# Two gate chunks as a unit of seven products, branch products inside the last attention steps, and three reorderings

## The chip, the cores and the metric

One core of a Trainium2 chip runs the whole program in one launch. The metric is the device time in microseconds (us): the median of several runs. A profile of one further execution, taken by the hardware profiler, says what each engine did. The engines are TensorE (PE; its weight loads are listed as PEld), VectorE (DVE), ScalarE (ACT), GpSimdE (POOL) and SyncE (SP), whose queue issues nearly all transfers. Each engine works through its own list of instructions in order.

## The reference, cut to what matters

One layer of a streaming encoder, 1024 frames, width 1024, in float32:

```
h  = rmsnorm(x, norm_mix_g);  z = h @ w_in
qa, fa, ia, ga, qb, kb, vb, gate_a, gate_b = split(z)
oa = hgrn2_mixer(qa, fa, ia, ga, ...)                 # 4 heads of 128
ob = band_attention(qb, kb, vb, ...)                  # 8 heads of 64, a chunk of 64 frames sees itself and 8 before
merged = sigmoid(gate_a) * (oa @ w_branch_a) + sigmoid(gate_b) * (ob @ w_branch_b)
x = x + merged @ w_out
x = x + (silu(h2 @ w_ffn_gate) * (h2 @ w_ffn_up)) @ w_ffn_down      # h2 = rmsnorm(x)
x = x + sigmoid(h3 @ w_ple_gate) * (p @ w_ple_proj)                 # h3 = rmsnorm(x)
```

The two gates have 16 chunks of 128 columns together (0 to 7 for gate_a, 8 to 15 for gate_b).

## The kernel before, in words

**Number format.** Nearly every large product is made of three matrix products of split operands: a float32 tile is rounded to a short form (`hi`, a CAST on ACT) and the rest is kept (`lo`, a subtraction on DVE or POOL). `gemm` (line 102) issues hi times hi, hi times lo and lo times hi. A product of a weight chunk (128 columns) with an activation of 512 frames and K = 1024 is 8 x 3 = 24 matmuls of 128x512; with K = 512 (the branch products) it is 12.

**Stages.** `units` computes pairs of chunks of z by a scheme of seven half-size products instead of eight (`strassen`): 7 x 4 x 3 = 84 matmuls for two chunks and 1024 frames, where the plain way takes 96. The list `JOBS` says which chunks: pairs of gate chunks ('gate'), a head's q and f ('head') and output gates ('out'). The results of a gate unit get a sigmoid and are stored to DRAM (`gate_done`, `gate_keep`). Then `hgrn_mix` works on the first mixer while plain products (gate chunks 0, 1, 4, 5 and v) fill PE between its steps. Then comes `attention`, then `branches` (products with w_branch_a and w_branch_b, multiplied by gates), `out_proj`, the feed-forward stages and `ple`, whose end writes the output.

**The attention loop** has 32 steps n = 0 to 31 (a pair of heads and a block of 128 frames each) and two more to empty the pipeline. Even and odd n go over the two pairs of a half. In step n, in the order of the code:

- `stage(n-1, 1)`: the second head of the step before is normalized: RECIPROCAL and TENSOR_SCALAR on DVE.
- `next(feed)`: a filler, six 128x512 matmuls of other work.
- `scores(n)`: 12 matmuls of 64 rows for both heads, then on DVE four reductions with bias (the profile calls them CUSTOM_DVE_ANT_0, the program order ISA).
- `stack(n+1)`: two transposes for the next step, two ACTIVATEs on ACT and two SCALAR_TENSOR_TENSORs on DVE, which make q and k of scores(n+1).
- `next(feed)`: a second filler.
- in odd n, `pv(n-3)` and `pv(n-2)`: products with v (128*64 tiles), copied out by ACT.
- `pt(n-1, 1)`, `stage(n, 0)`, `stage(n, 1)` (the two Exp on ACT), `pt(n-1, 0)`, `stage(n, 0)` (RECIPROCAL on DVE, then a scaling ACTIVATE on ACT): pt is five transposes of the normalized scores and two copies of them, one by ACT and one by DVE.

The fillers are first the q, k projections of the attention itself (`attn_in`; 56 pulls are left when the loop begins, so that they last through n = 27), then gate chunks 2 and 3 in the plain way (`gate`, 16 pulls of six matmuls; 12 of them fall into n = 28 to 33). Operations through `self.V`, `self.A`, `self.G`, `self.load` and `self.mul` keep the order in which the code is written, engine by engine; each list is worked through in order.

**The branch products** need the first mixer's output, which was stored to DRAM: `branch_load` loads four tiles of 128x1024, `split` makes hi (ACT) and lo (DVE) of each. Before, `branch_first` does this from n = 32 on, beside the last gate fillers, and `branches` starts after them. `tile()` products of the first source are TENSOR_TENSORs with a gate tile loaded by `gate_load`.

**The last outputs**: in `ple`, `last(u, ps, sp)` takes the last product's four blocks, the fourth in two parts of 256 frames. `out` is a stream of steps: a multiplication by `rb` (DVE), a sigmoid (ACT), a multiplication (DVE), an addition (POOL, or DVE for the last part) and the store.

Of the kernel before, what the change touches and what calls it, by code (L numbers as in the profile page):

```python
# [24 lines left out]
STEPS = (NFF // 2 + 1) // 2  # L25
EPS = 1e-6
# [9 lines left out]
PLAIN = 6  # L36
FIRSTS = (0, 1, 4, 5)
JOBS = (('gate', 6), ('head', 1), ('gate', 8), ('head', 2), ('gate', 10), ('head', 3), ('gate', 12), ('gate', 14), ('out', 0), ('out', 2))
# [36 lines left out]
class Trunk:  # L75
# [532 lines left out]
    def attn_in(self):  # L608

        nc = self.nc  # L610
        late = []

        def scale():
            two, b, ps, ss = late.pop(0)
            qk = self.small(HALF, tag="qk")
            self.V.tensor_tensor(
                qk[:, :].rearrange("p (a d) -> p a d", d=64), ps[:, :].rearrange("p (a d) -> p a d", d=64),
                ss[:, :].unsqueeze(2).to_broadcast([P, 8, 64]), ALU.mult)
            for i in range(2):
                self.qk[2 * two + i, b] = qk[:, 256 * i:256 * i + 256]  # L620

        for two in range(2):
            ws = self.weights(4, ahead=0)
            for b in range(8):
                pss = []
                for n, _ in enumerate(self.tokens(ws, (b,), pss)):
                    if b == 7:
                        self.weights(0, ahead=n + 1 if two == 0 else 2, direct=True)
                    if n < 3:
                        yield 1296  # L630
                    if n == 0 and late:
                        scale()
                (ps,) = pss
                sq = self.small(HALF, tag="qk")
                self.A.activation(sq, ps, AF.Square)
                ss = self.small(8)
                self.V.tensor_reduce(ss, sq[:, :].rearrange("p (a d) -> p a d", d=64), axis=AX.X, op=ALU.add)
                self.V.tensor_scalar(ss, ss, 1.0 / 64, self.epsv[:, b:b + 1], ALU.mult, ALU.add)
                self.G.tensor_tensor(ss, ss, self.mhalf[:, 0:8], ALU.pow)
                late.append((two, b, ps, ss))  # L640
                yield 1296
        self.scale = scale
# [78 lines left out]
    def attention(self):  # L721
# [3 lines left out]
        feed = chain(self.feed, self.gate(ahead=3), self.gate(ahead=2))  # L725
# [38 lines left out]
        for n in range(whole + 2):  # L764
# [8 lines left out]
            drain(stack(n + 1))  # L773
            next(feed, None)
            if n % 2:
                pv(n - 3)
                pv(n - 2)
            pt(n - 1, 1)
# [11 lines left out]
            if n == whole:  # L790
                while self.queue:
                    self.rest()
                self.queue = None
                tail = self.branch_first()
            if n >= whole:
                next(tail)
            yield 0
        for x in feed:
            next(tail, None)
            yield x  # L800
        drain(tail)
        self.pinned = True


    def gate(self, ahead=AHEAD):
        (w,) = self.weights(1, ahead=ahead)
        t = self.slot()
        self.gates.append(t)
        for half in range(2):
            stream = self.feature(w, self.u, half, piece=2)  # L810
            if self.scale:
                yield next(stream)
                self.scale()
                self.scale = None
            ps = yield from stream
            hs = slice(half * HALF, half * HALF + HALF)
            self.nc.vector.tensor_tensor(t[:, hs], ps, self.rb[:, hs], ALU.mult)
            yield 1296
# [218 lines left out]
    def branch_first(self):  # L1037
        self.weights(0, ahead=3)
        raws = self.branch_load(self.od)
        yield  # L1040
        yield
        self.osrc = []
        for i, raw in enumerate(raws):
            self.osrc.append(self.split(raw))
            yield
        self.keep_heads(self.ob, self.obd, [2, 3])
        self.bgates = []
        self.gate_load()
        for t in self.gates:
            self.A.activation(t, t, AF.Sigmoid)  # L1050
        self.bgates += self.gates

    def gate_load(self):
        if len(self.bgates) < 2 * KC:
            for _ in range(2):
                t = self.slot(late=len(self.bgates) > 3)
# [3 lines left out]
    def branches(self):  # L1060
# [11 lines left out]
        for dd in range(4):  # L1072
# [6 lines left out]
            for i in range(2):  # L1079
                c = 2 * dd + i  # L1080
                for half in range(2):
                    hs = slice(half * HALF, half * HALF + HALF)
                    ps = yield from self.feature(w, src, half, off=i * HALF)
# [807 lines left out]
    def ple(self):  # L1891
# [53 lines left out]
        def last(u, ps, sp):  # L1945
            for _ in range(max(0, min(2, len(todo) - u))):
                drain(todo.pop(0))
            while u == 3 and todo:
                drain(todo.pop(0))
            stream = out(2 * u, h0, ps, V if u == 3 and sp.start else G, sp, late=False)  # L1950
            next(stream)
# [68 lines left out]
    def run(self):  # L2020
        tc, d = self.tc, self.d
        order = []
        order += [d["fm"][i] for i in range(2)] + [d["tm"][i] for i in range(4)] + [d["fm"][2 + c] for c in FIRSTS]
        order += [d["wv"][i] for i in range(4)]
        order += [d["qk"][i] for i in range(8)]
        order += [d["fm"][2 + c] for c in (2, 3)] + [d["ba"][i] for i in range(4)] + [d["bb"][i] for i in range(4)]
# [11 lines left out]
        with ExitStack() as es:  # L2038
# [9 lines left out]
            self.gates = []  # L2048
            self.hg, self.ended, self.pend, self.qk, self.bias, self.ob = {}, [], [], {}, {}, []
            self.oa = [None] * 4  # L2050
            with ExitStack() as xs:
# [24 lines left out]
            with ExitStack() as xs:  # L2076
                self.late = xs.enter_context(tc.tile_pool(name="late", bufs=6, reuse_waits="tile"))
                drain(self.branches())
# [109 lines left out]
def layout(i):  # L2188
# [7 lines left out]
    d["fm"] = np.concatenate([cq[:1], cf[:1], cz[:PLAIN]])  # L2196
# [48 lines left out]
```

## Time and profile before

| | |
|---|---|
| median of 3 runs | 1539.32 us (1539.03 to 1540.14) |
| profiled execution | 1538.07 us, its span 1536.3 us |
| PE busy | 1515.4 us (99%), 7704 matmuls |
| DVE, ACT, POOL busy | 1102.7, 660.7, 630.1 us |
| TensorE clock granted | 0.999 |
| steps n = 0 to 31 of the attention, start of scores | 432.21 us (n = 0) to 607.92 us (n = 31) |
| the last two products with v end the loop at | 620.77 us (start) |

The share of PE is nearly the whole span, but a matmul's end is modelled: one that is listed with 389 ns is followed by the next after some 227 ns, so short waits of 0.1 to 0.3 us between matmuls hide behind a "busy" PE. They show only in the distance between starts. Rows of the timeline below give the start, the duration, the engine, the line, the operation, and what it writes and reads; "x12" are so many instructions merged into one row.

### The profile page before, as it was taken

The numbers are of one execution on the slowest core, as the hardware profiler recorded it, in microseconds if no ns is written. First come the engines' busy times: TensorE is split into PE (matmuls) and PEld (weight loads), VectorE is DVE, ScalarE is ACT, GpSimd is POOL, SyncE is SP. The second block draws the span as 40 slices with busy tenths as digits, with TensorE's granted clock in tenths as the row PEclk, the third lists the DMA queues.
The fourth block names the chain that finished last, engine by engine and source line by source line (L and its number), as shares of the span: only waits on it lengthen the run. The fifth ranks groups of instructions, "written<-read, shape, count | busy, mean of one in ns | idle before, by whom it ended". The sixth has DMA issues, their size and how long they took to land.

```text
span 1536.3 us, 20676 instructions
## 1 busy us (share of the span) xinstructions
PE 1515.4 (99%) x7704; PEld 1248.4 (81%) x7704; DVE 1102.7 (72%) x1597; ACT 660.7 (43%) x1104; POOL 630.1 (41%) x349
## 2 busy tenths in 40 slices
PE   8999999999999999999999999999999999999998
PEld 6888888888777878888888888888888888888886
DVE  5777774776767667348888877777777667756678
ACT  6633333434367677412575322222222224456452
POOL 4243333010334222254203666665555545545446
PEclk9999999999999999999999999999999999999999
DMA  5544444798443434866345344443233288775325
GB/s 200 200 164 144 144 151 151 266 300 290 153 83 69 121 66 118 293 184 201 124 162 182 115 118 127 124 124 105 103 103 104 104 321 309 284 269 179 124 102 199
DMA packets 97044, 256.56 MB, mean 167 GB/s; under 512 B 10032, under 2 KB 14896, under 8 KB 96432
## 3 DMA queue, kind: packets, MB, share of 16 engines
q1 hardware_dynamic: 90400, 239.51, 44.6%
q0 software_dynamic: 6400, 15.73, 6.2%
q8 instruction: 60, 0.98, 0.2%
q14 instruction: 40, 0.33, 0.1%
q10 hardware_dynamic: 144, 0.02, 0.0%
HBM read 193.08 MB, written 93.59 MB: 187 GB/s over the span
## 4 chain that ended last, share of the span: by engine, by line
PE 91%; DVE 5%; issue 1%; ACT 1%; DMA 1%; POOL 0%; SPq 0%; ACTq 0%; DVEq 0%; POOLq 0%
PE pm L102 88%; DVE s L72 4%; PE pm L105 3%; DVE m L72 0%; DMA s<-in_x 0%; ACT s L72 0%; DVE q L72 0%; POOL wl L72 0%; DMA wr<-in_qk 0%; ACT m L72 0%; DVE s L337 0%; ACT wh L142 0%; DVE wlo L72 0%; DVE s L234 0%; ACT t L72 0%
## 5 line engine op out<-in xcount | busy, mean ns | idle before, releaser
L102 PE MATMUL pm<-s,whi 128*128 128x512 f32 x1792 | 552.3, 389 | 0.6 <-DVE t L72 0.6
L102 PE MATMUL pm<-s,wh 128*128 128x512 f32 (+1 forms) x1584 | 491.9, 391 | 7.8 <-ACT wh L142 5.3
L102 PEld LDWEIGHTS pm<-s,whi 128*128 128x128 f32 x1792 | 336.2, 188 | 71.2 <-DVE t L72 1.4
L102 PEld LDWEIGHTS pm<-s,wh 128*128 128x128 f32 x1584 | 295.3, 188 | 70.7 <-ACT wh L142 5.2
L102 PE MATMUL pm<-s,wlo 128*128 128x512 f32 x896 | 348.6, 389 | 0.0
L72 DVE TENSOR_TENSOR s<-s,s 128x512 f32<-128x512 f32 (+3 forms) x236 | 285.7, 1241 | 53.5 <-ACT s L72 39.8
L102 PE MATMUL pm<-s,wl 128*128 128x512 f32 x792 | 308.4, 389 | 0.5 <-POOL wl L150 0.5
L150 POOL TENSOR_TENSOR wl<-wr,wh 128x1024 fp32r<-128x1024 f32 (+2 forms) x72 | 177.9, 2477 | 221.4 <-ACT wh L142 215.0
L72 DVE TENSOR_TENSOR t<-pm,t 128x512 f32<-128x512 f32 x158 | 108.9, 689 | 133.2 <-PE pm L102 110.4
L142 ACT CAST wh<-wr 128x1024 fp32r<-128x1024 f32 (+2 forms) x106 | 106.5, 1006 | 213.6 <-PE pm L102 94.3
L102 PEld LDWEIGHTS pm<-s,wlo 128*128 128x128 f32 x896 | 168.2, 188 | 34.7
L102 PE MATMUL pm<-wh,s 128*128 128x512 f32 x512 | 180.7, 407 | 0.0
L102 PEld LDWEIGHTS pm<-s,wl 128*128 128x128 f32 x792 | 148.9, 188 | 32.2 <-POOL wl L150 1.2
L72 POOL TENSOR_TENSOR wlo<-wr,whi 128x512 fp32r<-128x512 f32 (+1 forms) x63 | 132.3, 2107 | 67.5 <-ACT whi L72 58.4
L72 POOL TENSOR_TENSOR wlo<-q,whi 128x512 fp32r<-128x512 f32 x62 | 100.0, 1613 | 139.7 <-ACT whi L72 75.5
L72 POOL TENSOR_TENSOR m<-m,mhalf 128x8 f32<-128x8 f32 (+1 forms) x24 | 35.0, 1459 | 210.3 <-DVE m L72 210.3
L72 ACT CAST whi<-q 128x512 fp32r<-128x512 f32 (+1 forms) x93 | 70.5, 758 | 106.9 <-PE pm L102 87.1
L72 ACT CAST s<-s 128x1024 fp32r<-128x1024 f32 (+1 forms) x94 | 90.3, 980 | 58.1 <-DVE s L72 31.7
L72 POOL TENSOR_TENSOR s<-t,rb 128x512 f32<-128x512 f32 x44 | 71.2, 1619 | 98.6 <-ACT t L72 98.6
L102 PEld LDWEIGHTS pm<-wh,s 128*128 128x128 f32 x512 | 96.2, 188 | 18.3
L102 PE MATMUL pm<-wl,s 128*128 128x512 f32 x256 | 100.0, 391 | 0.0
L72 ACT ACTIVATE t<-s 128x512 f32<-128x512 f32 x44 | 27.9, 633 | 159.4 <-DVE s L72 155.4
(152 smaller groups left out, 1757.9 us busy)
## 6 DMA issues: line engine op xcount, KB each, us to landing
s<-d SPq DMA_DIRECT2D x81, 512.0 KB, 6.4
d<-s SPq DMA_DIRECT2D x87, 256.0 KB, 2.3
wr<-d SPq DMA_DIRECT2D x36, 512.0 KB, 3.4
d<-s SPq DMA_DIRECT2D x32, 512.0 KB, 4.4
d<-t SPq DMA_DIRECT2D x46, 256.0 KB, 2.3
wr<-in_sg SPq DMA_DIRECT2D x22, 512.0 KB, 4.3
wr<-in_su SPq DMA_DIRECT2D x22, 512.0 KB, 4.9
s<-in_x SPq DMA_DIRECT2D x21, 512.0 KB, 8.5
```

The costliest lines, as they stand in the source:

```text
L72: return lambda *a, **k: self.trunk.order(op(*a, **k), self.key)
L102: return self.order(self.nc.tensor.matmul(*a, **k))
L105: return self.order(self.nc.tensor.transpose(*a, **k))
L142: self.nc.scalar.copy(hi[:, c], raw[:, c])
L150: rest.tensor_tensor(lo[:, c], raw[:, c], f32(hi[:, c]), ALU.subtract)
```

## The change

1. Gate chunks 2 and 3 leave the attention and become a unit of seven products at the head of `JOBS`; `gate` and its fillers go. Their results take the way of the other gate units, through DRAM.
2. In the loop, `pv` stands directly behind `scores`, ahead of `stack` and the second filler.
3. The second filler is left out in n = 29, 30, 31. In n = 28 there is nothing left to pull, and from n = 29 on the fillers are the first branch products, by two K pieces (six matmuls) at a pull: 3 pulls in n = 29 to 31, 4 in n = 32 and 33.
4. The tiles of the first mixer are loaded at n = 22; their splits stand at the ends of the steps n = 24, 26, 27 and 28, in the fixed order of ACT and DVE. Four gate tiles are loaded at the end of n = 28.
5. In `last`, the first multiplication of the last part stands ahead of what is left of the part before.

```
-PLAIN = 6
+SPLITS = (24, 26, 27, 28)
-JOBS = (('gate', 6), ('head', 1), ...
+JOBS = (('gate', 2), ('gate', 6), ('head', 1), ...
...
-        self.scale = scale
+        scale()
...
-        feed = chain(self.feed, self.gate(ahead=3), self.gate(ahead=2))
+        feed = self.feed
...
-            drain(stack(n + 1))
-            next(feed, None)
             if n % 2:
                 pv(n - 3)
                 pv(n - 2)
+            drain(stack(n + 1))
+            if n < whole - 3 or n >= whole:
+                next(feed, None)
             pt(n - 1, 1)
...
-            if n == whole:
+            if n == whole - 10:
+                raws = self.branch_load(self.od)
+            if n in SPLITS:
+                raw = raws[len(self.osrc)]
+                hi, lo = self.slot(F32R), self.slot(F32R)
+                self.A.copy(hi, raw)
+                self.V.tensor_tensor(lo, raw, f32(hi[:, :]), ALU.subtract)
+                self.osrc.append((hi, lo))
+            if n == whole - 4:
                 while self.queue:
                     self.rest()
                 self.queue = None
-                tail = self.branch_first()
-            if n >= whole:
-                next(tail)
+                self.gate_load()
+                self.gate_load()
+                self.branch = self.branches()
+                feed = chain(feed, self.branch)
             yield 0
-        for x in feed:
-            next(tail, None)
-            yield x
-        drain(tail)
-        self.pinned = True
+        self.keep_heads(self.ob, self.obd, [2, 3])
...
-    def gate(self, ahead=AHEAD):
-    ...
-    def branch_first(self):
-    ...
-                t = self.slot(late=len(self.bgates) > 3)
+                t = self.slot(late=len(self.bgates) > 5)
...
-                    ps = yield from self.feature(w, src, half, off=i * HALF)
+                    ps = yield from self.feature(w, src, half, off=i * HALF, piece=2)
...
+            stream = out(2 * u, h0, ps, V if u == 3 and sp.start else G, sp, late=False)
+            if u == 3 and sp.start:
+                next(stream)
             while u == 3 and todo:
                 drain(todo.pop(0))
-            stream = out(2 * u, h0, ps, V if u == 3 and sp.start else G, sp, late=False)
-            next(stream)
+            if not (u == 3 and sp.start):
+                next(stream)
             next(stream)
...
-                drain(self.branches())
+                drain(self.branch)
```

**PE in the step n = 3**, the first with products with v. In the names, pm is a bank of PSUM, eye the unit matrix of a transpose, wh and wl a weight's hi and lo, 64x128 are products with v, 128x256 scores and 128x512 fillers. Before:

```order
L102 MATMUL pm_4008<-s_3768,m_3971 128x256
L105 MATMUL pm_4021<-eye,m_3976 128x128 x2
L102 MATMUL pm_3947<-wh_3597,s_192 128x512
L102 MATMUL pm_3947<-wl_3596,s_192 128x512
L102 MATMUL pm_3947<-wh_3597,s_193 128x512
L102 MATMUL pm_3947<-wh_3597,s_200 128x512
L102 MATMUL pm_3947<-wl_3596,s_200 128x512
L102 MATMUL pm_3947<-wh_3597,s_201 128x512
L102 MATMUL pm_4041<-m_3939,s_2888 64x128
L102 MATMUL pm_4041<-m_3931,s_2888 64x128
L102 MATMUL pm_4045<-m_3992,s_2889 64x128
L102 MATMUL pm_4045<-m_3984,s_2889 64x128
```

Now:

```order
L102 MATMUL pm_4152<-s_3912,m_4115 128x256
L102 MATMUL pm_4165<-m_4083,s_3032 64x128
L102 MATMUL pm_4165<-m_4075,s_3032 64x128
L102 MATMUL pm_4169<-m_4136,s_3033 64x128
L102 MATMUL pm_4169<-m_4128,s_3033 64x128
L105 MATMUL pm_4173<-eye,m_4120 128x128 x2
L102 MATMUL pm_4091<-wh_3741,s_192 128x512
L102 MATMUL pm_4091<-wl_3740,s_192 128x512
L102 MATMUL pm_4091<-wh_3741,s_193 128x512
L102 MATMUL pm_4091<-wh_3741,s_200 128x512
L102 MATMUL pm_4091<-wl_3740,s_200 128x512
L102 MATMUL pm_4091<-wh_3741,s_201 128x512
```

The products with v moved from behind the filler to behind the scores, and the filler now touches the transposes of pt.

**DVE from the end of step n = 27 into n = 28**: the DVE copies of pt, the two RECIPROCALs of step 27, the TENSOR_SCALAR that normalizes its second head, and the first reduction of scores(28). Before:

```order
L72 COPY m_5987<-pm_5993 128x256
L72 COPY m_6001<-pm_6007 128x256
L72 RECIPROCAL m_5997<-m_5997 128x1
L72 RECIPROCAL m_5999<-m_5999 128x1
L72 TENSOR_SCALAR s_5939<-s_5939,m_5999 128x640
L72 ISA m_6049,m_6050<-pm_6033,m_5013 128x384
```

Now, where the TENSOR_TENSOR of 128x1024 is the lo of the third split, which reads the CAST s_6173 of ACT:

```order
L72 COPY m_6147<-pm_6153 128x256
L72 COPY m_6161<-pm_6167 128x256
L72 RECIPROCAL m_6157<-m_6157 128x1
L72 TENSOR_TENSOR s_6174<-s_5706,s_6173 128x1024
L72 RECIPROCAL m_6159<-m_6159 128x1
L72 TENSOR_SCALAR s_6099<-s_6099,m_6159 128x640
L72 TENSOR_TENSOR m_6179<-pm_5981,m_6143 128x512
L72 ISA m_6197,m_6198<-pm_6181,m_5181 128x384
```

And ACT in the same place, now: the two Exp of step 27, a copy of pt, the scaling of the first head, the new CAST, and the two ACTIVATEs of the stack:

```order
L72 ACTIVATE m_6095,m_6157<-m_6095,m_6096 128x640
L72 ACTIVATE s_6099,m_6159<-s_6099,m_6100 128x640
L72 COPY m_6161<-pm_6162 128x384
L72 ACTIVATE m_6095<-m_6095,m_6157 128x640
L72 CAST s_6173<-s_5706 128x1024
L72 ACTIVATE s_3912<-pm_6205,cols 128x128
L72 ACTIVATE m_6208<-pm_6205,ones 128x128
```

Between the two RECIPROCALs there is now a subtraction that waits for the CAST, and the CAST stands behind the scaling of the first head. Steps 24, 26 and 28 have the same.

**PE at the border of steps 27 and 28**: the last transposes of pt, then the scores. Before:

```order
L105 MATMUL pm_5993<-eye,s_5864 128x128 x2
L105 MATMUL pm_6002<-eye,m_5860 128x128 x3
L105 MATMUL pm_6007<-eye,m_5860 128x128 x2
L102 MATMUL pm_6026<-s_133,wh_5833 128x512
L102 MATMUL pm_6026<-s_134,wh_5833 128x512
L102 MATMUL pm_6026<-s_133,wl_5832 128x512
L102 MATMUL pm_6026<-s_149,wh_5833 128x512
L102 MATMUL pm_6026<-s_150,wh_5833 128x512
L102 MATMUL pm_6026<-s_149,wl_5832 128x512
L102 MATMUL pm_6033<-s_3766,m_5946 128x384
```

Now:

```order
L105 MATMUL pm_6153<-eye,s_6020 128x128 x2
L105 MATMUL pm_6162<-eye,m_6016 128x128 x3
L105 MATMUL pm_6167<-eye,m_6016 128x128 x2
L102 MATMUL pm_6181<-s_3910,m_6130 128x384
L102 MATMUL pm_6183<-s_3910,m_6130 128x384
```

The filler between the two is gone; the second filler of n = 28 is gone too.

More of the change, by code (lines that the diff above doesn't have):

```diff
@@ L35 @@
 AHEAD = 3
-PLAIN = 6
 FIRSTS = (0, 1, 4, 5)
-JOBS = (('gate', 6), ('head', 1), ('gate', 8), ('head', 2), ('gate', 10), ('head', 3), ('gate', 12), ('gate', 14), ('out', 0), ('out', 2))
+JOBS = (('gate', 2), ('gate', 6), ('head', 1), ('gate', 8), ('head', 2), ('gate', 10), ('head', 3), ('gate', 12), ('gate', 14), ('out', 0), ('out', 2))
 C_MIX, C_FFN, C_PLE, C_ON, C_GQ, C_GK, C_LB = 0, 8, 16, 24, 25, 26, 27
@@ L793, in attention @@
                 self.queue = None
-                tail = self.branch_first()
-            if n >= whole:
-                next(tail)
+                self.gate_load()
+                self.gate_load()
+                self.branch = self.branches()
+                feed = chain(feed, self.branch)
             yield 0
-        for x in feed:
-            next(tail, None)
-            yield x
-        drain(tail)
-        self.pinned = True
-    def gate(self, ahead=AHEAD):
[L806 to L818, printed above, removed]
+        self.keep_heads(self.ob, self.obd, [2, 3])
     def gate_first(self, c):
@@ L1035, in branch_load @@
         return raws
-    def branch_first(self):
[L1038 to L1051, printed above, removed]
     def gate_load(self):
@@ L2022, in run @@
         order = []
-        order += [d["fm"][i] for i in range(2)] + [d["tm"][i] for i in range(4)] + [d["fm"][2 + c] for c in FIRSTS]
+        order += [d["fm"][i] for i in range(2)] + [d["tm"][i] for i in range(4)] + [d["fm"][2 + i] for i in range(len(FIRSTS))]
         order += [d["wv"][i] for i in range(4)]
         order += [d["qk"][i] for i in range(8)]
-        order += [d["fm"][2 + c] for c in (2, 3)] + [d["ba"][i] for i in range(4)] + [d["bb"][i] for i in range(4)]
+        order += [d["ba"][i] for i in range(4)] + [d["bb"][i] for i in range(4)]
         self.sums, self.osums = {}, {}
@@ L2047, in run @@
             self.r = self.rb = self.epsv = None
-            self.gates = []
             self.hg, self.ended, self.pend, self.qk, self.bias, self.ob = {}, [], [], {}, {}, []
             self.oa = [None] * 4
+            self.osrc, self.bgates = [], []
             with ExitStack() as xs:
@@ L2195, in layout @@
     cq, cf, cg, cz = columns(qa), columns(fa), columns(ga), np.concatenate([columns(g_a), columns(g_b)])
-    d["fm"] = np.concatenate([cq[:1], cf[:1], cz[:PLAIN]])
+    d["fm"] = np.concatenate([cq[:1], cf[:1], cz[list(FIRSTS)]])
     pick = {"head": lambda n: [cq[n], cf[n]], "gate": lambda n: [cz[n], cz[n + 1]], "out": lambda n: [cg[n], cg[n + 1]]}
```

## The prediction

> **What bounds the kernel now.** I read the page first: its engine rows say who is busy.
>
> ```profile
> PE 1515.4 (99%) x7704; PEld 1248.4 (81%) x7704; DVE 1102.7 (72%) x1597; ACT 660.7 (43%) x1104; POOL 630.1 (41%) x349
> ```
>
> PE is the bound, so the time is its products, plus what it loses between them. The view by windows then tells the two stages apart that the change touches; its columns are the window, then busy us (instructions) of PE, PEld, DVE, ACT and POOL, the clock, the DMA share and GB/s. The first row lies in the units, the second in the attention.
>
> ```profile
> 120.00:160.00 40.00, 40.00 (x178) 33.10 (x178) 31.22 (x38) 13.18 (x20) 15.35 (x10) 1.00 0.43 152
> 560.00:600.00 40.00, 40.00 (x350) 32.70 (x349) 30.10 (x104) 29.69 (x68) 13.33 (x9) 1.00 0.37 80
> ```
>
> In both DVE works 30 of 40 us and PE is listed as full. The timeline shows what a product really takes: twelve 128x512 matmuls start from the first of these rows to the second.
>
> ```profile
> 626.00 0.62 PE L102 MATMUL pm<-s,wh 128*128 128x512 f32 x2
> ...
> 628.72 0.62 PE L102 MATMUL pm<-s,wh 128*128 128x512 f32 x2
> ```
>
> 2.72 us / 12 = 0.2267 us each, not the listed length. Now PE in the steps n = 28 (scores at 589.49) and n = 29 (at 594.80) up to n = 30 (at 602.62), the transposes from the unit matrix being stack (x2) and pt (x5), the x40 the products with v:
>
> ```profile
> 589.49 1.15 PE L102 MATMUL pm<-s,m 64*128 64x384 f32 x12
> ...
> 590.57 0.44 PE L105 MATMUL pm<-eye,m 128*128 128x128 f32 x2
> ...
> 590.76 0.71 PE L102 MATMUL pm<-s,wh 128*128 128x512 f32 x2
> ...
> 592.24 0.71 PE L105 MATMUL pm<-eye,s 128*128 128x128 f32 x5
> ...
> 593.25 0.71 PE L102 MATMUL pm<-s,wh 128*128 128x512 f32 x2
> ...
> 594.80 1.15 PE L102 MATMUL pm<-s,m 64*128 64x384 f32 x12
> ...
> 595.88 0.44 PE L105 MATMUL pm<-eye,m 128*128 128x128 f32 x2
> ...
> 596.08 0.71 PE L102 MATMUL pm<-s,wh 128*128 128x512 f32 x2
> ...
> 597.65 2.40 PE L102 MATMUL pm<-m,s 128*64 128x128 f32 x40
> ...
> 599.98 0.77 PE L105 MATMUL pm<-eye,s 128*128 128x128 f32 x5
> ...
> 601.05 0.71 PE L102 MATMUL pm<-s,wh 128*128 128x512 f32 x2
> ...
> 602.62 1.15 PE L102 MATMUL pm<-s,m 64*128 64x384 f32 x12
> ```
>
> From start to start: scores 1.08, stack 0.20, a filler 1.48 ahead of pt but 1.57 ahead of scores or products with v, products with v 2.33, pt 1.01 (1.07 behind products with v). Six products alone are 1.36: each change of the tile's form costs 0.1 to 0.2. Nothing waits long here, because two fillers, 2.9 us of a step of 5.3 or 7.8 us, cover the chain on ACT and DVE. That chain, in step 27 and the start of 28:
>
> ```profile
> 588.64 0.85 ACT L72 ACTIVATE m<-m,m 128x640 f32<-128x640 f32 x1
> ...
> 589.46 0.83 ACT L72 ACTIVATE s<-s,m 128x640 f32<-128x640 f32 x1
> ...
> 590.27 0.48 ACT L72 COPY m<-pm 128x384 f32<-128x384 f32 x1
> ...
> 590.42 0.16 DVE L72 RECIPROCAL m<-m 128x1 f32<-128x1 f32 x1 [0.64 <-ACT s L72]
> ...
> 590.62 0.55 DVE L72 TENSOR_SCALAR s<-s,m 128x640 f32<-128x640 f32 x1
> 590.63 0.85 ACT L72 ACTIVATE m<-m,m 128x640 f32<-128x640 f32 x1
> ...
> 591.09 0.55 DVE L72 CUSTOM_DVE_ANT_0 m<-pm,m 128x384 f32<-128x384 f32 x1
> ...
> 591.37 0.38 ACT L72 ACTIVATE s<-pm,cols 128x128 fp32r<-128x128 f32 x1
> ...
> 593.31 0.35 DVE L72 SCALAR_TENSOR_TENSOR s<-pm,cols,s 128x128 fp32r<-128x128 f32 x1
> ...
> 593.84 0.68 DVE L72 TENSOR_TENSOR m<-pm,m 128x512 f32<-128x512 f32 x1
> ...
> 594.43 0.75 DVE L72 COPY m<-pm 128x256 f32<-128x256 f32 x2
> ...
> 595.10 0.22 DVE L72 RECIPROCAL m<-m 128x1 f32<-128x1 f32 x2
> ```
>
> From start to start, ACT: the second Exp 0.81, a copy of pt 0.36, the scaling 0.74. DVE: RECIPROCAL 0.20, TENSOR_SCALAR 0.47, the four reductions 2.22, the two of the stack 0.53, the scaling of q and k 0.59, the copies of pt 0.67.
>
> **The change part by part.** *The unit.* 96 plain products go, 84 come: 12 x 0.2267 = -2.72 us. A unit has the room: in its window DVE works 31 of 40, ACT and POOL less, DMA 0.43, and PE runs without a gap. The four stores and two more gate tiles to load ride on that DMA share; the removed evacuations of the gates on DVE and their sigmoids on ACT lay beside PE. All at nothing; if a unit waited somewhere, it would show as a period above 84 x 0.2267 = 19.0 us.
>
> *Products with v behind scores.* Per odd step before: 1.08 + 0.20 + 1.57 + 2.33 + 1.07 = 6.25; now scores, products with v, stack, filler, pt: 1.08 + 2.33 + 0.20 + 1.48 + 1.01 = 6.10, so -0.15. No row has scores directly followed by products with v; I take the price of scores followed by transposes, the nearest. Its ends: nothing at all (-0.35) or twice as much (+0.05). What they need is there: the copies of pt began at 594.43 and take 0.75, so they end at 595.18, ahead of 595.88. 15 odd steps (3 to 31): -2.25 us, between -5.2 and +0.8.
>
> *The splits.* This is the costly part. Where they come from, two rows, CASTs and subtractions of 128x1024:
>
> ```profile
> 618.28 2.00 ACT L230 CAST s<-s 128x1024 fp32r<-128x1024 f32 x2
> ...
> 621.49 3.49 DVE L231 TENSOR_TENSOR s<-s,s 128x1024 fp32r<-128x1024 f32 x3
> ```
>
> 1.00 and 1.16 us each. The subtraction stands on DVE ahead of the second RECIPROCAL and TENSOR_SCALAR; it waits for a CAST which ACT reaches only after a copy of pt and the scaling. So TENSOR_SCALAR comes 0.36 + 0.74 + 1.00 + 1.16 = 3.26 us later, and with it all reductions of the next scores. Behind steps 24 and 26 a step with products with v follows, where pt comes late:
>
> ```profile
> 582.65 0.98 DVE L72 TENSOR_SCALAR s<-s,m 128x640 f32<-128x640 f32 x1
> ...
> 586.57 0.68 DVE L72 TENSOR_REDUCE m<-m 128x8 f32<-128x512 f32 x1
> ...
> 586.86 0.77 PE L105 MATMUL pm<-eye,s 128*128 128x128 f32 x5
> ```
>
> 582.65 + 3.26 + 0.47 + 0.2 to the first transpose = 586.6, where PE, 0.3 earlier by two odd steps, wants it at 586.55: hidden, wait 0.1. But DVE goes on 2.9 us late, with no second wait to spare, and then the fillers are gone. On the clock of before:
>
> - Step 27: reductions from 586.4, stack 588.6 to 589.1, TENSOR_REDUCE and its follower 0.9, copies of pt to 590.7, RECIPROCAL; ACT scales the first head 590.9 to 591.65, CAST to 592.65; subtraction to 593.85, TENSOR_SCALAR 594.05 to 594.55.
> - Step 28 on PE: pt ends 587.6, no filler; scores need the stack's result of 589.1: wait 1.5. After 1.3 us of scores and stack pt needs TENSOR_SCALAR: from 590.4 to 594.8, wait 4.4.
> - DVE: scaling 0.59, reductions 2.22, stack 0.53, to 597.9; copies to 598.55; scaling of the first head to 599.5, CAST to 600.5, subtraction to 601.7, TENSOR_SCALAR 601.9 to 602.4.
> - Step 29: pt, one filler, PE at 597.4; scores at 598.0, wait 0.6; products with v to 601.4, stack; pt wanted at 601.6, had at 602.65, wait 1.0.
> - Steps 30 and 31: one filler each, no split; DVE has 4.5 us a step and PE 3.9 or 6.2: waits of 0.1, 0.15 and 0.65. Then two fillers cover again.
>
> Sum of waits 8.5 us. Its ends: 0, if all is covered, and 13, if each of four splits shows its 3.26.
>
> *Other moved work.* Four loads of 512 KB move from n = 32 to n = 22 and four gate loads to n = 28, ahead of branch weights on SP's queue.
>
> ```profile
> s<-d SPq DMA_DIRECT2D x81, 512.0 KB, 6.4
> ```
>
> At 6.4 us from issue to landing, both have two steps (over 11 us) to their first reader; a late one would add to the split's wait. POOL takes over lo parts of branch weights from DVE, and works 13 of 40 us here. The branch products only change places: from n = 29 on they fill what the gates filled, 42 instead of 72 products within the loop, the rest later.
>
> *The last outputs.*
>
> ```profile
> 1523.43 9.43 POOL L72 TENSOR_TENSOR s<-s,s 128x512 f32<-128x512 f32 x8 [0.67 <-DVE s L72]
> ...
> 1532.80 0.42 DVE L72 TENSOR_TENSOR s<-s,s 128x256 f32<-128x256 f32 x1
> ```
>
> DVE's last addition ends at 1533.22; without the multiplication (0.46) and a sigmoid (0.37) in series it ends 0.8 earlier. But POOL's row of eight additions ends at 1532.86, and its last store stands ahead on SP's queue, so the last store gains little: -0.05, between -0.8 and 0.
>
> Sum: -2.72 - 2.25 + 8.5 - 0.05 = +3.5 us on 1538.07 us, the profiled execution, which lies 1.25 below the median of the runs: 1541.6 there, 1542.8 as a median.
>
> **The rivals.**
>
> *The clock drops in the long wait.* After the last matmul the granted clock halves:
>
> ```profile
> 1530.00:1533.00 3.00, 0.11 (x1) 0.00 (x0) 1.92 (x5) 0.74 (x2) 2.86 (x3) 1.00 0.48 180
> 1533.00:1536.30 3.30, 0.00 (x0) 0.00 (x0) 0.22 (x1) 0.00 (x0) 0.00 (x0) 0.75 0.46 159
> ```
>
> A mean of 0.75 over 3.3 us is half clock from 1534.65 on, 4.5 us after PE ended at 1530.1; my longest wait is 4.4. If it dropped, the next 3.3 us of products (pt, filler, scores) would take twice as long, less 1.4 us of the waits that follow: +1.9, 1544.7. [...]
>
> *DVE catches up.* It idles 10 of 40 us in the attention. If the 2.9 us of step 26's split were gone by step 27's end, step 28 would wait 0 for the stack and 3.2 for pt, and less later: about 5.0 instead of 8.5, 1539.3, no change. For it: that idle share. Against: the idle time lies where ACT is waited for, and the subtractions wait for ACT too.
>
> *Nothing waits* (the other side). The place is pt in steps 28 and 29. Should the subtraction start as early as ACT's scaling, as the other subtractions between two RECIPROCALs do (their casts are steps old), DVE's chain would fit: -5.0, 1534.3. It decides the sign where the waits stay below 5.0 us, and below 1.9 the gain passes 0.2%. Against it: the order on both engines.
>
> **How the numbers follow.** 0.2% of 1539.3 is 3.1 us, about what a measurement of this kernel can tell. My forecast, waits of 6 to 10.5 us, 0.60, own range 1540.3 to 1544.8; of this 0.37 are slower, 0.23 within 0.2%. Clock drop 0.13, slower. DVE catches up 0.15, nearly all within. Nothing waits 0.10, faster; 0.02 for anything else faster. So faster 0.14, within 0.2% 0.36, slower 0.50. The range leaves out "nothing waits" and takes in higher waits and products with v at their better end: 1536 to 1546.
>
> **What would show it.** In the profile after: units of 19.0 us; odd steps shorter by 0.15; PE waiting on DVE's TENSOR_SCALAR some 4 us in step 28 and 1 us in 29, and on ACT's CAST behind DVE; the last store hardly earlier. No wait above 1 us in steps 28 to 31 would prove me wrong, as would a branch product that waits for a load.

## The result, and the profile after

| | before | changed | changed, second time |
|---|---|---|---|
| median | 1539.17 us (6 runs) | 1545.73 us (6 runs, 1543.11 to 1546.5) | 1542.99 us (5 runs, 1542.92 to 1546.19) |
| ratio to before, 95% interval | | 1.0038 [1.0025, 1.0051] | 1.0037 [1.0025, 1.005] |
| profiled execution, span | 1538.07, 1536.3 us | 1546.48, 1544.7 us | 1544.69, 1542.9 us |

The kernel became slower by 0.4%, 12 matmuls fewer notwithstanding. The engine row of its page:

```profile
PE 1517.0 (98%) x7692; PEld 1252.4 (81%) x7692; DVE 1107.8 (72%) x1603; ACT 661.5 (43%) x1109; POOL 634.2 (41%) x353
```

PE is busy 1.6 us longer with fewer matmuls (7704 before): some of them ran at a lower clock (0.50 from 362.67 to 366.08, from 615.26 to 618.67 and from 830.30 to 833.71 us). Where the 8.4 us between the two spans arose is seen when the same event is looked up in both timelines. First the row of 32 small products in the mixer, then the scores of n = 0, of the changed kernel:

```profile
357.38 0.70 PE L102 MATMUL pm<-s,s 128*32 128x32 f32 x32
...
361.73 1.16 PE L102 MATMUL pm<-s,s 128*64 128x64 f32 x16 [2.06 <-DVE s L72]
```

Before, these two stood at 338.84 and 341.06. With the starts of scores(0), scores(25), the last product with v (622.90 and 644.29) and the last matmul (1529.83 and 1538.10) the difference splits up:

| stretch | longer by | what is in it |
|---|---|---|
| up to the 32 small products | +18.54 | 84 products of the unit, 19.04, less 0.7 of waits in the first 20 us, and 0.2 elsewhere |
| to scores(0) | +3.63 | a wait of 2.1 and 1.5 of halved clock in the mixer |
| to scores(25) | -1.27 | 11 odd steps by -0.15, and +0.4 in step 12 |
| to the last product with v | +0.49 | 36 products fewer (-8.16), 4 odd steps (-0.6), so 9.2 of waits and slow clock |
| to the last matmul | -13.12 | 60 products fewer (-13.60), +0.5; the clock is halved once more, at 830.30 us |
| to the end | +0.10 | the last outputs |

The sum is 8.37 us. Of the 9.2 us, 5.6 are listed as idle time of PE and some 1.5 are slow clock; the rest is not listed. Most of it lies in step 28, where the forecast had it. The timeline of step 28 in the changed kernel (scores had begun at 609.30):

```profile
611.08 0.75 DVE L72 COPY m<-pm 128x256 f32<-128x256 f32 x2
611.55 0.44 PE L105 MATMUL pm<-eye,m 128*128 128x128 f32 x2 [0.39 <-DVE m L72]
611.74 0.15 DVE L72 RECIPROCAL m<-m 128x1 f32<-128x1 f32 x1
611.93 0.83 ACT L72 ACTIVATE m<-m,m 128x640 f32<-128x640 f32 x1 [0.81 <-DVE m L72]
612.67 1.03 ACT L72 CAST s<-s 128x1024 fp32r<-128x1024 f32 x1
613.73 1.23 DVE L72 TENSOR_TENSOR s<-s,s 128x1024 fp32r<-128x1024 f32 x1 [1.83 <-ACT s L72]
614.87 0.16 DVE L72 RECIPROCAL m<-m 128x1 f32<-128x1 f32 x1
615.06 0.55 DVE L72 TENSOR_SCALAR s<-s,m 128x640 f32<-128x640 f32 x1
615.76 1.30 PE L105 MATMUL pm<-eye,s 128*128 128x128 f32 x5 [3.78 <-DVE s L72]
```

Read it from the bottom: PE's transposes of pt waited 3.78 us for TENSOR_SCALAR, which stood behind the split's subtraction, which waited 1.83 us for ACT's CAST, which stood behind the scaling. And five transposes that took 0.71 us before now take 1.30. The windows around that wait give the granted clock (the fraction behind the engines' columns):

```profile
612.00:615.50 3.50, 0.00 (x0) 0.00 (x0) 1.74 (x3) 2.22 (x4) 1.83 (x2) 0.97 0.54 145
615.50:619.00 3.50, 3.24 (x14) 3.07 (x15) 3.21 (x13) 1.93 (x4) 0.00 (x0) 0.55 0.55 107
619.00:622.00 3.00, 3.00 (x38) 2.46 (x38) 1.17 (x4) 2.50 (x5) 0.00 (x0) 1.00 0.01 3
```

From the end of the wait on PE worked 2.91 us at half clock (0.50 from 615.76 to 618.67).

### The profile page after: what moved, and what is told of

Same layout as the page of the kernel before. It is cut to its first block, busy times and chain, and to the rows that moved or that the text cites. A ratio compares the mean times of both kernels' runs of the same rounds, so it can differ in the third digit from the quotient of the medians.

```text
span 1544.7 us, 20689 instructions
## 1 busy us (share of the span) xinstructions
PE 1517.0 (98%) x7692; PEld 1252.4 (81%) x7692; DVE 1107.8 (72%) x1603; ACT 661.5 (43%) x1109; POOL 634.2 (41%) x353
## 4 chain that ended last, share of the span: by engine, by line
PE 91%; DVE 5%; DMA 1%; ACT 1%; issue 1%; SPq 0%; POOL 0%; DVEq 0%; ACTq 0%; POOLq 0%
PE pm L102 89%; DVE s L72 3%; PE pm L105 3%; DMA m<-d 0%; ACT wh L142 0%; DMA s<-in_x 0%; DVE m L72 0%; ACT s L72 0%; DMA wr<-in_fm 0%; ACT m L72 0%; DMA wr<-in_wv 0%; DVE s L337 0%; SPq L97 0%; DVE s L234 0%; DVE wl L72 0%
## 5 line engine op out<-in xcount | busy, mean ns | idle before, releaser
L102 PE MATMUL pm<-s,whi 128*128 128x512 f32 x1848 | 568.9, 389 | 0.0
L102 PE MATMUL pm<-s,wh 128*128 128x512 f32 (+1 forms) x1520 | 472.2, 392 | 6.8 <-ACT wh L142 5.2
L102 PEld LDWEIGHTS pm<-s,whi 128*128 128x128 f32 x1848 | 346.8, 188 | 72.0 <-DVE t L72 0.2
L102 PE MATMUL pm<-s,wlo 128*128 128x512 f32 x924 | 359.4, 389 | 0.0
L102 PEld LDWEIGHTS pm<-s,wh 128*128 128x128 f32 x1520 | 284.5, 189 | 66.6 <-ACT wh L142 5.2
L72 DVE TENSOR_TENSOR s<-s,s 128x512 f32<-128x512 f32 (+3 forms) x240 | 293.3, 1251 | 60.7 <-ACT s L72 47.0
L102 PE MATMUL pm<-s,wl 128*128 128x512 f32 (+1 forms) x760 | 296.4, 390 | 0.5 <-POOL wl L150 0.5
L102 PEld LDWEIGHTS pm<-s,wlo 128*128 128x128 f32 x924 | 173.5, 188 | 36.0
L102 PEld LDWEIGHTS pm<-s,wl 128*128 128x128 f32 x760 | 143.3, 189 | 31.0 <-POOL wl L150 1.2
L72 POOL TENSOR_TENSOR wlo<-wr,whi 128x1024 fp32r<-128x1024 f32 (+1 forms) x65 | 136.0, 2099 | 68.0 <-ACT whi L72 58.9
```

Source lines behind the costliest of these rows:

```text
L72: return lambda *a, **k: self.trunk.order(op(*a, **k), self.key)
L102: return self.order(self.nc.tensor.matmul(*a, **k))
```

## Experiments

Each is compared with runs of the kernel before on the same chip. Theory S says that the place of the split's subtraction makes the waits of steps 26 to 29, rival C that the missing fillers alone do; theory L says that an operation of DVE on SBUF tiles that meets a subtraction of POOL ends only when POOL's has ended.

| run | median us | ratio to before |
|---|---|---|
| e1 changed kernel again | 1542.99 | 1.0037 [1.0025, 1.005] |
| e2 products with v alone | 1538.66 | 1.0004 [0.9995, 1.0013] |
| e3 subtractions later | 1537.65 | 0.9993 [0.9984, 1.0002] |
| e4 splits in steps 16 to 22 | none: the program deadlocks | |
| e5 splits in steps 20 to 26 | 1539.54 (10 runs, without one of 5671.16) | 1.0006 [0.9997, 1.0015] |
| e6 e3, lo by DVE in steps 8 to 12 | 1548.80 | 1.0069 [1.0057, 1.0082] |
| e7 e3, lo by DVE at the end | 1537.94 | 0.9996 [0.9987, 1.0005] |
| e8 e3, branch products from n = 32 | 1540.83 | 1.0015 [1.0006, 1.0024] |
| e9 e3, POOL in halves | 1536.83 | 0.9984 [0.9975, 0.9993] |
| e10 e9, splits in steps 20 to 24 | 1535.80 | 0.9977 [0.9968, 0.9986] |
| e11 e3, products with v where they were | 1538.95 | 0.9997 [0.9989, 1.0006] |
| e12 e10, last multiplications to SBUF | 1536.10 | 0.9983 [0.9973, 0.9992] |

**e1, the changed kernel again**, no edit.

> The changed kernel once more, for a second profile. Theory L (the lone long wait in the mixer, 2.2 us at 361.73, came because the last v weight landed early enough for POOL's subtraction to run beside a pair of DVE additions, which then took 3.46 instead of 1.29 us): that is a matter of when a transfer lands, so it may be missing here; without it the mixer stretch is 3.6 us shorter (2.1 of wait and 1.5 of halved clock) and the profiled execution about 1543; with it 1546.5. Rival F (the wait is fixed by the order of the program): it stands in every profile of this program, at 2.1 to 2.2 us. Wait for TENSOR_SCALAR in step 28: 3.8 to 3.9 us and a halved clock behind it in either case.

The mixer's wait is missing here; scores(0) begins at 451.64, 2.7 us earlier, though the 32 small products came 0.9 us later. The timelines say why. In the changed kernel's first profile, DVE's two additions and POOL's subtraction:

```profile
358.12 3.46 DVE L72 TENSOR_TENSOR s<-s,s 128x512 f32<-128x512 f32 x2 [0.55 <-PE pm L102]
358.17 2.86 POOL L72 TENSOR_TENSOR wl<-wr,wh 128x1024 fp32r<-128x1024 f32 x1 [17.24 <-ACT wh L142]
```

and in the second:

```profile
359.02 1.29 DVE L72 TENSOR_TENSOR s<-s,s 128x512 f32<-128x512 f32 x2 [0.55 <-PE pm L102]
360.47 2.37 POOL L72 TENSOR_TENSOR wl<-wr,wh 128x1024 fp32r<-128x1024 f32 x1 [18.63 <-ACT wh L142]
```

POOL starts when the last v weight has landed and been cast. In the thirteen profiles of this study it started 0.10 to 2.57 us behind the end of the 32 small products; DVE's second addition starts 0.66 behind it. In the two profiles where POOL was ahead of it (0.10 in the first profile, 0.40 in e11) that addition took 2.85 us and PE waited 2.1; in the eleven others (0.78 and later) it took 0.69 and PE waited for nothing there. Theory L holds: in one and the same program the wait comes and goes with the landing. Whether the unit in front makes an early landing more likely is not shown; the two profiles without it (before and e2) have 2.14 and 2.33 us. The expected 1543 came as a median; the profiled execution itself took 1544.69, with a wait of 1.6 us in step 12 instead of 1.2. Step 28 waited 3.8 us for TENSOR_SCALAR again, with half clock in it and behind it, 6.8 us in all.

**e2, products with v alone**, on the kernel before:

```
-            drain(stack(n + 1))
-            next(feed, None)
             if n % 2:
                 pv(n - 3)
                 pv(n - 2)
+            drain(stack(n + 1))
+            next(feed, None)
```

> The kernel before with one edit: products with v directly behind scores. Theory of the prediction: 0.15 us less in each of 15 odd steps, 2.25 us in all, 1537.0 beside 1539.2. Rival (the saved change of tile form is given back as a wait, since pt of the step now follows the stack after one filler only): less than 0.7 us in all, and waits before pt that the kernel before does not have.

Each odd step became 0.13 to 0.17 us shorter, step 29 for one went from 7.82 to 7.66 us, as forecast. But the whole did not. What PE waits for between 494 and 630 us, where the kernel before has only a wait of 0.8 us in step 12:

```profile
PE pm L102 <- DVE m L72: 1.3, 1, 1.3
PE pm L105 <- DVE s L72: 0.8, 1, 0.8
```

The first is in step 12, the second is the last pt, which now has no filler ahead of it. The windows of step 12:

```profile
494.00:497.40 3.40, 2.08 (x16) 1.27 (x15) 2.81 (x7) 3.02 (x8) 3.16 (x2) 1.00 0.03 6
497.40:500.80 3.40, 3.40 (x12) 2.71 (x12) 3.11 (x12) 1.21 (x3) 1.70 (x2) 0.53 0.32 47
```

Half clock again, behind a gap of only 1.3 us: step 12 took 8.58 us against 6.48 before. So the 2.1 us of the odd steps up to scores(31) were given back as 2.1 in step 12, and from there to the last matmul the kernel took 0.9 us longer, in this execution; the medians are the same.

**e3, the subtraction behind the next step's stack**:

```
                 self.A.copy(hi, raw)
-                self.V.tensor_tensor(lo, raw, f32(hi[:, :]), ALU.subtract)
                 self.osrc.append((hi, lo))
+                rests = [(lo, raw, f32(hi[:, :]))]
...
             drain(stack(n + 1))
+            for r in rests:
+                self.V.tensor_tensor(*r, ALU.subtract)
+            rests = []
```

> The changed kernel with the four subtractions of the splits moved from between the two RECIPROCALs to behind the next step's SCALAR_TENSOR_TENSORs of the stack; casts, steps and fillers stay. Theory S (the place of the subtraction, which makes TENSOR_SCALAR wait for the cast): the wait of 3.9 us in step 28 falls below 1.2, the clock stays full, 5 to 7 us less than the changed kernel, 1539 to 1541. Rival C (the cover is gone, with no second filler from n = 28 on, and the chain shows by itself): at least 2.5 us of wait stays in step 28, and the time stays above 1543.

5.3 us less than e1, within the 5 to 7 that were expected; the time lies below the 1539 to 1541, which were reckoned from the slower first set. PE's waits from 584 to 640 us, first of the changed kernel, then of e3:

```profile
PE pm L105 <- DVE s L72: 4.4, 2, 3.8
PE pm L105 <- ACT m L72: 0.8, 2, 0.5
PE pm L105 <- DVE m L72: 0.4, 1, 0.4
```

```profile
PE pm L105 <- DVE s L72: 0.8, 1, 0.8
PE pm L102 <- DVE s L72: 0.6, 1, 0.6
PE pm L105 <- ACT m L72: 0.4, 1, 0.4
PE pm L105 <- DVE m L72: 0.3, 1, 0.3
PE pm L102 <- DVE m L72: 0.2, 1, 0.2
```

The clock stayed at 1.00 from 600 to 625 us, and scores(25) to the last product with v took 48.7 instead of 54.4 us. Same casts, same fillers, same 1.2 us on DVE: only the place changed. Of these 5.7 us, 4.5 lie ahead of scores(31), and that is theory S. The other 1.2 lie behind it, where no split stands: there TENSOR_SCALAR took 2.36 us beside POOL in the changed kernel and 0.76 in e3. What is left in step 28, 1.3 us of listed waits, is rival C's share.

**e4, the splits in steps 16, 18, 20 and 22** of the changed kernel, the tiles loaded at n = 14, gave no time: in this order the program deadlocks. The expectation, 1537 to 1540, is untested; e5 asks the same question four steps later.

**e5, the splits in other steps**, the subtraction still between the RECIPROCALs:

```
-SPLITS = (24, 26, 27, 28)
+SPLITS = (20, 22, 24, 26)
...
-            if n == whole - 10:
+            if n == whole - 14:
```

> The changed kernel with the splits at the ends of n = 20, 22, 24 and 26 (tiles loaded at n = 18) in place of 24, 26, 27 and 28; the subtraction stays between the RECIPROCALs. Theory S (a late TENSOR_SCALAR costs only where PE has nothing else): in the changed kernel the splits behind 24 and 26 cost 0.2 us each in the step after the next, so four of them cost about 1 us here, and step 28 keeps only what the run with the later subtraction has there, 2 us: 1537 to 1539. Rival (each split costs its 3.26 us wherever it stands, because DVE does not catch up): waits of 8 us or more in steps 20 to 30, 1543.

Against e3 the stretches behind the four splits grew by 0.3, 0.6, 0.5 and 0.1 us, and step 28 by 0.4. So the same late TENSOR_SCALAR costs about 0.5 us where two fillers and products with v follow, and with the clock 4.3 to 5.0 us in step 28, where nothing follows (10.46 and 11.16 us in the changed kernel's profiles, 6.18 in e3). The median lies 0.5 us above what was expected, 1.9 above e3, of which the profiles show 1.1.

**e6, lo parts of steps 8 to 12 by DVE**:

```
-                        self.weights(0, ahead=n + 1 if two == 0 else 2, direct=True)
+                        self.weights(0, ahead=n + 1 if two == 0 else 2, direct=two == 1)
```

> The kernel with the later subtractions, and one more edit: the lo parts of the four weights that are fetched in steps 8 to 12 are made by DVE, as queued halves, not by POOL. Theory L (POOL's subtraction of 128x1024 holds up DVE's small operations on SBUF: TENSOR_SCALAR 128x8 took 1.23 instead of 0.23 us in step 12 of the run with products with v alone): the wait of 1.4 us in step 12 falls below 0.4, and no clock drop follows it, so 1 to 2.5 us less than the run with the later subtractions, 1535.2 to 1536.7, and a narrower spread. Rival (the wait in step 12 comes from elsewhere, or DVE has no room): the same time or more.

A miss by 12 us. The edit brought a wait of its own, so the time says nothing on theory L; the TENSOR_SCALAR of 128x8 itself took 0.23 us, as the theory has it. What DVE waits for between 508 and 528 us:

```profile
DVE wl L72 <- ACT wh L142: 6.6, 1, 6.6
```

The lo parts are called for before their weights have landed, so DVE, which works in order, stood 6.6 us at one of them, and three waits of PE of 2.3 to 2.7 us and half clock followed (the mean granted clock of this run is 0.995, that of e3 0.999). In e3, where POOL makes these parts, PE has no such wait in these steps.

**e7, lo parts by DVE at the end of the loop**: the queue of lo parts is emptied behind the loop, not at n = 28.

```
-                while self.queue:
-                    self.rest()
-                self.queue = None
                 self.gate_load()
...
+        while self.queue:
+            self.rest()
+        self.queue = None
         self.keep_heads(self.ob, self.obd, [2, 3])
```

> The kernel with the later subtractions, and one more edit: the queue of lo parts is kept to the end of the loop, so that DVE and not POOL makes the lo parts of the first branch weights. Theory L: TENSOR_SCALAR of steps 31 and 32, which took 2.36 us beside POOL's subtractions in the changed kernel and 0.76 in the run with later subtractions, takes 0.55; 0 to 1 us less. Rival: DVE, which has 4.5 us of work per step there, becomes later by its four halves of 0.64 us: 0.5 to 2 us more.

No difference from e3 (scores(25) to the last product with v 48.8 against 48.7). TENSOR_SCALAR took 0.55 us, as theory L has it, against 0.76 in e3, but in neither did PE wait for it in step 31.

**e8, branch products from n = 32**:

```
-                feed = chain(feed, self.branch)
+            if n == whole - 1:
+                feed = chain(feed, self.branch)
```

> The kernel with the later subtractions, and one more edit: the branch products begin at n = 32 and not at n = 29, so that no fillers stand in steps 28 to 31. Theory C (cover): DVE's 4.5 us of a step set the pace where PE has 2.3 us in an even step and 4.6 in an odd one, and the 18 matmuls (4.1 us) that covered it come later: 3 to 6 us more than the run with the later subtractions, 1540.5 to 1544. Rival (fillers in these steps only add to PE and the chain has room): within 1 us of it.

3.2 us more than e3, within the expected. PE's waits, 584 to 640 us:

```profile
PE pm L105 <- DVE s L72: 2.3, 2, 1.4
PE pm L102 <- DVE m L72: 2.0, 3, 0.9
PE pm L105 <- DVE m L72: 0.3, 1, 0.3
```

So the early start of the branch products is worth 2 to 3 us: they fill what the gates left.

**e9, POOL's subtractions in two halves inside the loop**:

```
-        rest.tensor_tensor(lo[:, c], raw[:, c], f32(hi[:, c]), ALU.subtract)
+        for x in range(a, b, HALF if self.halves else b - a):
+            c = slice(x, min(b, x + (HALF if self.halves else b - a)))
+            rest.tensor_tensor(lo[:, c], raw[:, c], f32(hi[:, c]), ALU.subtract)
```

> The kernel with the later subtractions, and one more edit: inside the attention loop POOL's subtractions for the lo parts of weights are issued as two of 128x512 (estimate: half of 2.4 us each) and not one of 128x1024. Theory L (a DVE operation from SBUF to SBUF ends only when the POOL operation beside it has ended; TENSOR_SCALAR 128x8 at the end of step 11 ended 0.04 us behind POOL's): it can now be held for at most 1.2 us, so the wait in step 12 falls from 1.4 to 0.2 to 1.0 us and the clock drops there seldom; 0.3 to 1.5 us less than the run with the later subtractions, 1536.2 to 1537.4. Rival (DVE is held for the whole stretch in which POOL has work): wait and time as in that run.

In step 12 of the changed kernel, DVE's small TENSOR_SCALAR beside POOL's subtraction, and PE's wait behind it:

```profile
516.04 2.38 POOL L72 TENSOR_TENSOR wl<-wr,wh 128x1024 fp32r<-128x1024 f32 x1 [0.61 <-ACT wh L142]
...
517.22 1.24 DVE L72 TENSOR_SCALAR m<-m,m 128x8 f32<-128x8 f32 x1
...
518.84 0.62 PE L102 MATMUL pm<-s,m 64*128 64x256 f32 x5 [1.18 <-DVE m L72]
```

and in e9 (four halves in one row):

```profile
511.48 5.03 POOL L72 TENSOR_TENSOR wl<-wr,wh 128x512 fp32r<-128x512 f32 x4 [1.39 <-ACT wh L142]
...
515.13 0.23 DVE L72 TENSOR_SCALAR m<-m,m 128x8 f32<-128x8 f32 x1
```

No wait above 0.2 us is left in step 12, and it takes 5.66 us instead of 6.89 in e3. Other operations are still held: TENSOR_SCALAR of 128x640 took 1.48 us at 508.18, beside one half. With this edit the interval lies below the kernel before; it overlaps that of e3.

**e10, all that helped**, on e9:

```
-SPLITS = (24, 26, 27, 28)
+SPLITS = (20, 21, 22, 24)
...
-            if n == whole - 10:
+            if n == whole - 14:
```

> All that helped together: later subtractions, splits at the ends of n = 20, 21, 22 and 24 (tiles loaded at n = 18), POOL's subtractions in halves inside the loop. Theory S with cover: no subtraction is left in steps 26 to 29, so the wait of 2.1 us in step 28 falls by about 1, the 0.7 in step 30 stays, and with the halves 1.5 to 3 us less than the run with the later subtractions: 1534.7 to 1536.2, 0.15 to 0.25% less than the kernel before. Rival (step 28 waits because it has no filler, whatever DVE did before): wait of 2 us stays, 1536.5 to 1538.

The fastest: 3 us below the kernel before, some 7 to 10 below the changed one. PE's waits, 584 to 640 us:

```profile
PE pm L105 <- DVE s L72: 1.0, 1, 1.0
PE pm L105 <- DVE m L72: 0.4, 1, 0.4
```

The first is step 28's: it stayed, so the rival has that much of it, though the step became 0.7 us shorter than in e3. The second is new, in step 26.

**e11, products with v back behind the second filler**, on e3:

```
-            if n % 2:
-                pv(n - 3)
-                pv(n - 2)
             drain(stack(n + 1))
...
             if n < whole - 3 or n >= whole:
                 next(feed, None)
+            if n % 2:
+                pv(n - 3)
+                pv(n - 2)
```

> The kernel with the later subtractions, with products with v back behind the second filler as in the kernel before. Theory: 15 odd steps longer by 0.15 us, less what the new order gave back (0.5 us more wait in step 12, a wait of 1 us before the last pt): 1 to 2.2 us more than the run with the later subtractions, 1538.7 to 1539.9. Rival (the new order gains nothing on the whole, as the run with it alone suggests): the same time within 0.7 us.

scores(0) to the last product with v takes 186.65 us against 184.23 in e3, but with six more products ahead of its end. To scores(31), with equal products, it is 173.25 against 172.20: the odd steps are 1.9 us longer, steps 12 and 28 together 0.9 shorter. In the profile the order gains 1.0 us, the lower end of what was expected. The medians, 1538.95 and 1537.65, come from different sets of runs, and their ratios to before overlap, so they don't settle it.

**e12, the last multiplications to SBUF**, on e10:

```
-            V.tensor_tensor(t, t, self.rb[:, at], ALU.mult)
+            g = self.slot()[:, :HALF][:, sp] if sp.stop - sp.start < HALF else t
+            V.tensor_tensor(g, t, self.rb[:, at], ALU.mult)
+            t = g
```

> The kernel with all that helped, and one more edit: the first multiplication of the last product's two parts writes to tiles of their own in SBUF, and not back into the one PSUM tile that both parts share. Theory T (the reordered multiplication gained nothing because it waits for the sigmoid of the other part, which writes the same tile): the second part's multiplication starts without the 0.43 us of idle time, DVE's last addition starts 0.4 to 0.9 us earlier after the last product (2.97 before), and the span from the last product to the end falls from 6.43 by 0.1 to 0.8 us. Rival (POOL's additions and the stores set the end): the addition is earlier, but the end stays within 0.1 us. In the median neither can be told from the kernel with all that helped.

In the changed kernel the second part's multiplication had waited for the other part's sigmoid:

```profile
1538.89 0.37 ACT L72 ACTIVATE pm<-pm 128x256 f32<-128x256 f32 x1 [2.02 <-DVE pm L72]
...
1539.29 0.43 DVE L72 TENSOR_TENSOR pm<-pm,rb 128x256 f32<-128x256 f32 x1 [0.43 <-ACT pm L72]
...
1541.07 0.42 DVE L72 TENSOR_TENSOR s<-s,s 128x256 f32<-128x256 f32 x1
```

In e12 the two follow each other, and then:

```profile
1527.80 0.76 DVE L72 TENSOR_TENSOR s<-pm,rb 128x256 f32<-128x256 f32 x2 [0.83 <-PE pm L102]
1528.71 2.20 DVE L72 TENSOR_TENSOR s<-s,s 128x256 f32<-128x256 f32 x3
1529.79 0.84 POOL L72 TENSOR_TENSOR s<-s,s 128x256 f32<-128x256 f32 x1 [0.36 <-DVE s L72]
```

Three operations that take 0.42 us each took 2.20: two of them ran beside POOL's additions. DVE's last addition starts 0.37 us earlier after the last matmul than in e10, but it ends 3.4 us after it, as before, and the program 6.66 us after it (6.43 in e10). The wait was real, but what replaced it, operations with both inputs in SBUF, meets POOL.

## Why the prediction was right, and where not

**The unit**: right. 18.54 us more in front, of which 84 x 0.2267 = 19.04 are products.

**Products with v**: the size per step was right (-0.15). The step that failed is the sum: 15 x -0.15 was entered in full, without asking what comes next. Step 12 already waited 0.8 us in the kernel before, for DVE; a PE that comes earlier waits longer there (1.2 and 1.6 us in the changed kernel's profiles, 1.3 and half clock in e2), and the last pt loses its cover.

**The splits**: the mechanism and its place held; e3 and e5 show it. The sum (8.5 forecast, 9.2 measured) is near in part by luck, since some 1.5 of the 9.2 are slow clock, and some are POOL's hold, both of which the forecast had at nothing. In both sums a moved product counts 0.2267; the 0.1 to 0.2 us that a filler's changes of form cost are left out. The composition did not hold. In step 28 the scores and the stack took 1.2 us longer from start to start than before (2.25 against 1.08) and pt waited 3.8, against 1.5 and 4.4; step 29 shows no wait, against 1.6, perhaps because the slow clock gave DVE time; and steps 30 to 33 list 1.4 of waits against 0.9. Of the rivals, "DVE catches up" and "nothing waits" did not come about.

**The clock**: the forecast took it as held, since its longest wait was 4.4 us and the clock in the one idle stretch of before fell after 4.5. In both profiles of the changed kernel it fell within the wait of 3.8, 3.3 us into it in the first and 1.4 us into it in the second. That rival, given 0.13, was what happened, and its time, 1544.7, lies between the two medians. The step that failed is the reading of one event as a threshold. For the 3.3 us of half clock in that rival's sum no row of before stands; in the first profile of the changed kernel it lasted 3.41 us, of which 2.91 behind the end of the wait, and in the second 6.8.

**POOL, at nothing**: wrong twice. In the changed kernel, in step 31:

```profile
629.92 4.73 POOL L72 TENSOR_TENSOR wl<-wr,wh 128x1024 fp32r<-128x1024 f32 x2 [16.10 <-ACT wh L142]
...
632.64 2.36 DVE L72 TENSOR_SCALAR s<-s,m 128x640 f32<-128x640 f32 x1
...
635.15 0.82 PE L105 MATMUL pm<-eye,s 128*128 128x128 f32 x5 [0.64 <-DVE s L72]
```

TENSOR_SCALAR, 0.55 us with nothing beside it, ended 0.35 us behind POOL's second subtraction, and PE waited for it. The clue stood in a row the prediction quoted without asking: TENSOR_SCALAR took 0.98 us at 582.65. The wait in step 12 of the kernel before is such a hold too: there the TENSOR_SCALAR of 128x8 took 1.25 us at 495.39. The mixer's wait of 2.1 us with 1.5 of half clock is the same hold; it struck by the landing of a weight, and no term allowed for it. Without it the profiled sum is 8.37 - 3.63 = 4.7 us, near the forecast 3.5. The second median, 1542.99, meets the forecast of 1542.8, and the first, 1545.73, lies outside 1540.3 to 1544.8 and inside 1536 to 1546. But e1's profile, which has no wait in the mixer, is still 6.6 us longer than before's: it has 0.9 more up to the small products, 0.5 more in step 12 and 0.7 more in step 28 than the first profile.

**The last outputs**: +0.1 for -0.05 forecast, but for another reason. DVE's last addition was to end 0.8 earlier; it ended 3.39 us after the last matmul, as before, because the multiplication that was moved ahead waited 0.43 us for ACT's sigmoid on the other half of its PSUM tile.

What tells the executions of 1543 us from those of 1546 us is not settled: a profile shows one of them, and the mixer's wait and the clock drops come and go. The mean granted clock fits in the first six runs (0.997 in the two of 1543 us, 0.995 and 0.996 in the others), but not in the second set, where the run of 1542.99 us has 0.995.

## What to carry to other kernels

When work is moved between the steps of an in-order engine, look at what the moved operation waits for, and at which instruction stands behind it: the same four subtractions of 1.2 us cost some 5 us between two RECIPROCALs and little behind the next step's stack. Put it where the following step has cover, and then ask what becomes the next wait, since a saving of tenths per step is easily given back at one place. Durations that differ between rows of the same shape are a finding: ask what ran beside the longer one before pricing a neighbour at nothing.

## What the runs showed of the hardware

**DVE and POOL.** In the two profiles of before and of the changed kernel, TENSOR_SCALARs and TENSOR_TENSORs of DVE that read only SBUF (s and m in the rows; pm is PSUM) ended only when the subtraction that POOL had begun before them had ended: TENSOR_SCALAR 128x8 0.03 us behind it (1.24 instead of 0.23), 128x640 0.35 behind (0.98 to 2.36 instead of 0.55), additions of 128x512 0.55 behind (2.85 instead of 0.69). Each profile has one exception, an addition of 128x1024 near its start (at 27.48 in the changed kernel, 1.21 us beside a subtraction begun at 27.32). The reductions of scores, which read PSUM, stayed at 0.55 and 0.48 beside POOL (at 600.12 and 599.71 in the changed kernel), and TENSOR_REDUCE of 128x8 at 0.69 us (at 516.50), though it reads SBUF alone. In step 12 of e9 shorter POOL instructions took the wait away: TENSOR_SCALAR 128x8 took 0.23 us there.

**The clock.** It fell to half within waits of 3.8 us in both profiles of the changed kernel and behind a wait of 1.3 us in e2 (0.53 from 497.4 to 500.8). In the mixer a wait of 2.06 us was followed by a granted clock of 0.58 in the next 4 us in the changed kernel (first row) and by 1.00 in e11 (second row):

```profile
362.00:366.00 4.00, 4.00 (x23) 3.22 (x22) 3.07 (x6) 0.36 (x1) 0.00 (x0) 0.58 0.97 332
```

```profile
362.00:366.00 4.00, 3.85 (x28) 3.32 (x29) 3.11 (x9) 0.36 (x1) 0.00 (x0) 1.00 0.97 264
```

So the length of a wait alone does not decide it. Step 28 in e1, where PE waited from 609.73 to 613.50, shows when it falls:

```profile
609.50:613.30 3.80, 0.24 (x2) 0.00 (x0) 1.94 (x6) 2.28 (x4) 2.07 (x2) 0.71 0.66 193
613.30:616.70 3.40, 3.20 (x13) 3.03 (x14) 3.11 (x13) 1.88 (x4) 0.00 (x0) 0.50 0.61 114
616.70:620.00 3.30, 3.30 (x31) 2.48 (x31) 1.46 (x5) 2.54 (x5) 0.00 (x0) 0.81 0.01 2
```

A mean of 0.71 over 3.80 us is half clock for 2.2 us, so it fell at 611.1, only 1.4 us into the wait, and stayed down for 6.8 us; the others within the kernel lasted 3.4 us, but for one of 6.8 in e6. The trace also records when the granted clock changes. In the first profile of the changed kernel it falls at 362.67, 615.26 and 830.30 us, in the second at 611.13 and 829.58, and within each profile the distances are whole multiples of 3.413 us (74, 63 and 64 times). In the first profile each of the three drops lasts 3.413 us. Why the mixer's wait was followed by one in the changed kernel and not in e11 is not shown. The drop at 830 us follows sixteen products of one column (1.84 us) and a wait of 0.26 us; it came in five of the thirteen profiles, and the nine 128x512 products behind it took 3.75 us from start to start, against 2.17 in e3.

In e2 PE is listed as busy for 2.08 of the 3.40 us ahead of the drop. What decides it besides the length of a wait is not settled here.
